# The layer norm ahead of the expert stage, with its last tile centred early and its mean spread beside the root

## The chip, the cores and the metric

One Trainium2 chip, one NeuronCore of it. The metric is the device time of one execution in microseconds; lower is better. Before the change, three runs gave 3672.79 us as the median (3670.61 to 3675.13).

## What is computed

Two blocks of a network on 512 tokens of width 1024, in float32. The first block has two layers, each with two SwiGLU feed-forward parts and a token mixer of gated MLP, differential attention and sparse attention. The second block is one layer: a second token mixer, a layer norm, an expert stage (PEER: 8 heads choose 16 of 16,384 experts for each token) and a last layer norm. The change concerns the first layer norm of the second block and the start of the expert stage behind it:

```python
def layer_norm(x, g, b):
    mu = jnp.mean(xf, axis=-1, keepdims=True)
    xc = xf - mu
    var = jnp.mean(xc * xc, axis=-1, keepdims=True)
    return xc * lax.rsqrt(var + LN_EPS) * g + b

x = layer_norm(DEEPNORM_ALPHA * x + m, ln1_g[l], ln1_b[l])   # m: the mixer's output
f = peer_ffn(x, ...)                                         # begins with q = x @ wq
```

## The kernel before

Activations lie transposed: `self.x[k]` (k = 0 to 7) holds 128 channels on the partitions and 512 tokens along the free axis. Sums over channels are therefore sums over partitions and over the eight tiles. Every float32 product is made of three matmuls of split operands: a weight tile is loaded into `raw` by SyncE's DMA queue, ScalarE rounds it into a high part (`wh`, line 260), VectorE subtracts to get the low part (`wl`, line 261), and activations are split in the same way into `yh` and `yl` (lines 266 and 267). `raw` has four buffers, `wh` and `wl` three each. A scheduler of the framework lays out each engine's queue at build time and sets the semaphores; on the chip each queue runs in that fixed order.

The stage around the change runs as follows.

- In `mix2`, the output projection gives one tile of 128 channels after another: 24 matmuls of 512 columns each (line 283), then VectorE adds the result to `ALPHA * x[d]` (line 1542). `centre` (lines 1244 to 1261) subtracts a provisional mean `cen`, which was taken from tiles 0 and 1, from each tile as it comes; ScalarE squares it (line 1258), and VectorE adds the tile and its square to the running tiles `csum` and `csq` (lines 1260 and 1261). Behind the last projection, three weight units of the expert stage's first product (`heads`, from `wq`) are loaded and split ahead of time (`unit`).
- `moments` (line 1263) lets PE sum `csum` and `csq` over the partitions with a column of ones, four matmuls of one column for each; a float32 matmul appears as two passes in the trace. VectorE works out mean `lnm` and variance `lnv` on 128x4 tiles, and `rsqrt` (line 318) makes the inverse root from a bit trick and three Newton steps, nine small instructions on `rst` and `rsy`.
- `normed` (line 1278) spreads two 512-token rows over all partitions by matmuls with the identity (`spread`, line 348): the inverse root `rsy` and the product of mean and root, `lnmr`. For each tile k, ScalarE makes `e = -g*lnmr + b` (line 1289), VectorE `y = x*g*rsy` (line 1291) and `x = y + e` (line 1293).
- In `peer`, ScalarE and VectorE split each normalized tile into `yh` and `yl`, and PE adds its nine matmuls (three heads, three parts each; `mm3`, lines 271 to 273) into three PSUM banks. Two of these banks come free only when the two spread rows have been read to the end. PE also transposes all tiles to token rows (32 matmuls of 128 columns, line 1780), which ScalarE copies out (line 1781); then it copies the heads' results (`x<-proj`, line 1610), which frees the banks for the dense expert products (line 283 again).

Of the kernel before, what the change touches and what calls it, by code (L numbers as in the profile page):

```python
# [10 lines left out]
F32 = mybir.dt.float32  # L11
# [4 lines left out]
AF = mybir.ActivationFunctionType  # L16
OP = mybir.AluOpType
AX = mybir.AxisListType

P = 128  # L20
S = 512
D = 1024
KT = D // P
NT = S // P
# [7 lines left out]
ALPHA = 2.0 ** 0.25  # L32
# [161 lines left out]
class Net:  # L194
# [58 lines left out]

    def unit(self, src, n=1024):
        nc = self.nc
        raw = self.rawp.tile([P, 1024], F32, name="raw", tag="raw")
        nc.sync.dma_start(raw[:, :n], src)
        h = self.wp.tile([P, 1024], F32R, name="wh", tag="wh")
        l = self.wp.tile([P, 1024], F32R, name="wl", tag="wl")
        nc.scalar.activation(h[:, :n], raw[:, :n], AF.Copy)  # L260
        self.latest = nc.vector.tensor_sub(l[:, :n], raw[:, :n], h[:, :n].bitcast(F32)).ins  # L261
        return h, l
# [997 lines left out]
                nc.vector.tensor_add(self.csum, self.csum if k > 1 else self.x[0], x)  # L1260
                nc.vector.tensor_add(self.csq, self.csq, sq)

    def moments(self):

        nc = self.nc
        ps = self.bank("stat")
        for i, v in enumerate((self.csum, self.csq)):
            for t in range(NT):
                nc.tensor.matmul(ps[:, i * NT + t:i * NT + t + 1], lhsT=v[:, t * P:(t + 1) * P],
                                 rhs=self.ones[:, :1], start=True, stop=True)  # L1270
        m, v, q = (self.sm(NT, n, bufs=1) for n in ("lnm", "lnv", "lnq"))
        nc.vector.tensor_scalar(m, ps[:, :NT], 1.0 / D, None, op0=OP.mult)
        nc.vector.tensor_scalar(v, ps[:, NT:2 * NT], 1.0 / D, LN_EPS, op0=OP.mult, op1=OP.add)
        nc.vector.tensor_mul(q, m, m)
        nc.vector.tensor_sub(v, v, q)
        return self.rsqrt(v, NT), m

    def normed(self, st, g, b, out, mk):

        nc = self.nc  # L1280
        r, m = st
        mr = self.sm(NT, "lnmr", bufs=1)
        nc.vector.tensor_mul(mr, m, r)
        rb, mb = self.spread(r), self.spread(mr)
        ng = self.sm(KT, "lnng", bufs=1)
        nc.vector.tensor_scalar(ng, g, -1.0, None, op0=OP.mult)
        for k in range(KT):
            e = mk("lne")
            nc.scalar.activation(e, mb, AF.Identity, scale=ng[:, k:k + 1], bias=b[:, k:k + 1])
            y = mk("lny")  # L1290
            nc.vector.scalar_tensor_tensor(y, self.x[k], g[:, k:k + 1], rb, op0=OP.mult, op1=OP.mult)
            o = out(k)
            nc.vector.tensor_add(o, y, e)
            yield k, o

    def mix2(self, begun):
        nc, A = self.nc, self.A
        X, begun = begun
        self.main = "T"
        vec = self.blk(name="vec2")  # L1300
        o = 0
        V = {}
        for n, w in (("convw", 62), ("convb", 2), ("nag", 2), ("nab", 2), ("pools", 2), ("convc", 6)):
            V[n] = vec[:, o:o + w]
            src = A[n]
# [218 lines left out]
        rb = self.layer_norm(H, 256)  # L1524
# [4 lines left out]
        for a in range(2):  # L1529
            y = self.t32("y")  # L1530
# [4 lines left out]
        attend(1)  # L1535

        Y = YB + YC + YA + YD
        for d in range(KT):
            ps = self.proj(A["wout2"][d], Y)
            if d == KT - 1:  # L1540
                heads = [self.unit(A["wq"][i].rearrange("p k m -> p (k m)")) for i in range(3)]
            nc.vector.scalar_tensor_tensor(self.x[d], self.x[d], ALPHA, ps, op0=OP.mult, op1=OP.add)
            self.centre(d - 1)
        self.centre(KT - 1)
        return self.moments(), heads

    def top16(self, vals, n, out, idx):

# [197 lines left out]
    def peer(self, out, begun):  # L1746
        nc, A = self.nc, self.A
# [5 lines left out]
        n, last, early = S - GT, len(BLOCKS) - 1, GT // P  # L1753
# [7 lines left out]
        ln = cst[:, 384:400].rearrange("p (a b) -> p a b", a=2)  # L1761
# [5 lines left out]
        XT = [self.cact] + [stage.tile([P, D], F32, name=f"xt{t}", tag=f"xt{t}") for t in range(1, NT)]  # L1767
        stats, heads = begun
        X, begun = [], [self.bank("proj") for _ in heads]
        for k, x in self.normed(stats, ln[:, 0], ln[:, 1], lambda k: self.x[k], self.t32):  # L1770
            X.append(self.new_pair())
            self.split(x, *X[k])
            c = slice(k * P, (k + 1) * P)
            for ps, (h, l) in zip(begun, heads):
                self.mm3(ps, h[:, c], l[:, c], *X[k], k == 0, k == KT - 1)
# [66 lines left out]
        while not over or kept % 2:  # L1842
            g = self.t32("hg")[:, GT:]
# [8 lines left out]
        for j in range(kept, NE):  # L1852
# [6 lines left out]
            hi, lo = (v[:, :n] for v in self.new_pair())  # L1859
# [6 lines left out]
        for i in range(4):  # L1866
            src = A["ln2"][i // 2, i % 2 * S:(i % 2 + 1) * S]
# [121 lines left out]
```

## Time and profile before

| | |
|---|---|
| median of three runs | 3672.79 us |
| the profiled execution | 3671.99 us |
| its span, first to last instruction | 3670.2 us |
| PE busy | 3554.5 us |
| VectorE (DVE) busy | 2394.7 us |
| ScalarE (ACT) busy | 1562.9 us |
| mean granted TensorE clock | 0.988 of full speed |

The profile is of one execution on the chip. PE is TensorE's matmuls, PEld its weight loads, DVE VectorE, ACT ScalarE, POOL GpSimd, and SPq, ACTq and POOLq the queues' own work (DMA issues). All moments are microseconds from the span's start; a duration behind an instruction is how long it ran. Matmuls overlap: of a row with eight matmuls the time runs from the first start to the last end. Idle time in brackets names what the engine waited for, and on which line that was made.

### The profile page before, as it was taken

How to read it: one execution, taken by the hardware profiler on the slowest of the kernel's cores; microseconds unless marked ns; L12 is line 12 of the kernel's file. 1: busy time of each engine (PE TensorE's matmuls, PEld its weight loads, DVE VectorE, ACT ScalarE, POOL GpSimd, SP SyncE). 2: the span in 40 equal slices, each digit the busy share in tenths (PEclk: the TensorE clock that was granted, in tenths of full speed). 3: DMA queues.
4: the chain of work that ended last, by engine and by line, in shares of the span. 5: the costliest groups of instructions: out<-in, count | busy, mean ns of one | idle time of the engine just before them, and what ended most of it. 6: DMA issues, size and time to landing. Idle time of an engine off the chain costs nothing. (4 is left out here: it accounts for less than half of the span.)

```text
span 3670.2 us, 49271 instructions
## 1 busy us (share of the span) xinstructions
PE 3554.5 (97%) x18265; PEld 3019.0 (82%) x18265; DVE 2394.7 (65%) x4791; ACT 1562.9 (43%) x2769; POOL 369.2 (10%) x358
## 2 busy tenths in 40 slices
PE   7999999999999999999999999899899999999998
PEld 6888876788888888767888887788899999988786
DVE  6555687665563334776533386699877667778787
ACT  4332366433233323465432263433667753334333
POOL 0000100000000001000000000021221134432220
PEclk9999999999999999999999999999999999999999
DMA  7666320266653333401333322265686879999995
GB/s 249 190 186 198 115 94 18 64 202 193 201 178 109 94 95 105 133 24 31 91 98 93 97 79 68 84 202 195 206 289 235 296 262 308 313 327 346 336 341 183
DMA packets 259665, 635.72 MB, mean 173 GB/s; under 512 B 82336, under 2 KB 117584, under 8 KB 256864
## 3 DMA queue, kind: packets, MB, share of 16 engines
q1 hardware_dynamic: 206368, 473.96, 40.1%
q0 software_dynamic: 39808, 140.52, 11.2%
q10 hardware_dynamic: 13248, 18.09, 1.3%
q8 instruction: 143, 2.34, 0.3%
q14 instruction: 98, 0.80, 0.1%
HBM read 591.32 MB, written 41.16 MB: 172 GB/s over the span
## 5 line engine op out<-in xcount | busy, mean ns | idle before, releaser
L260 ACT ACTIVATE wh<-raw 128x1024 fp32r<-128x1024 f32 (+2 forms) x620 | 645.3, 1043 | 1129.3 <-PE proj L283 880.6
L261 DVE TENSOR_TENSOR wl<-raw,wh 128x1024 fp32r<-128x1024 f32 (+2 forms) x620 | 744.1, 1201 | 508.4 <-ACT wh L260 370.1
L283 PE MATMUL proj<-yh,wh 128*128 128x512 f32 (+1 forms) x2744 | 644.7, 375 | 9.1 <-ACT hg L1839 4.2
L283 PE MATMUL proj<-yh,wl 128*128 128x512 f32 (+1 forms) x2744 | 629.1, 371 | 13.6 <-DVE wl L261 13.6
L283 PE MATMUL proj<-yl,wh 128*128 128x512 f32 (+1 forms) x2744 | 628.4, 370 | 0.0
L283 PEld LDWEIGHTS proj<-yh,wl 128*128 128x128 f32 x2744 | 506.4, 189 | 82.8 <-DVE wl L261 15.5
L283 PEld LDWEIGHTS proj<-yh,wh 128*128 128x128 f32 x2744 | 501.1, 189 | 85.0 <-ACT hg L1839 5.7
L283 PEld LDWEIGHTS proj<-yl,wh 128*128 128x128 f32 x2744 | 505.4, 189 | 67.5
L535 DVE SCALAR_TENSOR_TENSOR scr<-raw,cact 128x1024 bf16<-128x1024 f32 x128 | 156.7, 1224 | 136.3 <-DMA raw<-in_wada 136.0
L1822 PE MATMUL acc<-wl,yh 128*128 128x512 f32 x756 | 236.2, 394 | 2.7 <-DVE wl L261 2.6
L1822 PE MATMUL acc<-wh,yh 128*128 128x512 f32 x756 | 235.0, 392 | 3.6 <-ACT yh L266 2.1
L1822 PE MATMUL acc<-wh,yl 128*128 128x512 f32 x756 | 234.3, 391 | 0.3 <-DVE yl L267 0.3
L1737 POOL DMA_INDIRECT row<-in_purows,c x128 | 156.5, 1223 | 537.9 <-DVE row L1721 261.6
L667 DVE TENSOR_TENSOR ga<-sg,proj 128x512 f32<-128x512 f32 x88 | 60.5, 687 | 225.7 <-PE proj L283 223.2
L1737 POOL DMA_INDIRECT row<-in_pv,c x128 | 165.2, 1291 | 392.6 <-DVE vacc L1729 275.8
L272 PE MATMUL proj<-yl,wh 128*128 128x256 f32 (+1 forms) x552 | 177.0, 330 | 10.6 <-DVE yl L394 7.0
L273 PE MATMUL proj<-yh,wl 128*128 128x256 f32 (+1 forms) x552 | 174.6, 324 | 2.2 <-DVE wl L261 2.2
L1822 PEld LDWEIGHTS acc<-wl,yh 128*128 128x128 f32 x756 | 141.1, 188 | 38.4 <-DVE wl L261 9.5
L271 PE MATMUL proj<-yh,wh 128*128 128x256 f32 (+1 forms) x552 | 164.8, 328 | 7.8 <-ACT yh L640 6.3
L1822 PEld LDWEIGHTS acc<-wh,yh 128*128 128x128 f32 x756 | 142.1, 189 | 32.0 <-ACT yh L266 2.5
L1822 PEld LDWEIGHTS acc<-wh,yl 128*128 128x128 f32 x756 | 142.5, 189 | 31.4 <-DVE yl L267 1.0
L1729 DVE SCALAR_TENSOR_TENSOR vacc<-row,act,vacc 128x1024 f32<-128x1024 f32 x127 | 162.5, 1280 | 0.6
(465 smaller groups left out, 5166.7 us busy)
## 6 DMA issues: line engine op xcount, KB each, us to landing
raw<-in_wada SPq DMA_DIRECT2D x144, 512.0 KB
raw<-in_pu SPq DMA_DIRECT2D x128, 512.0 KB
raw<-in_pv SPq DMA_DIRECT2D x128, 512.0 KB
raw<-in_wg SPq DMA_DIRECT2D x84, 512.0 KB
raw<-in_wu SPq DMA_DIRECT2D x84, 512.0 KB
raw<-in_wd SPq DMA_DIRECT2D x64, 512.0 KB
gates<-st SPq DMA_DIRECT2D x20, 1024.0 KB
acts<-hg ACTq DMA_DIRECT2D x92, 192.0 KB
```

What stands on the lines that cost most here:

```text
L260: nc.scalar.activation(h[:, :n], raw[:, :n], AF.Copy)
L261: self.latest = nc.vector.tensor_sub(l[:, :n], raw[:, :n], h[:, :n].bitcast(F32)).ins
L271: mm(out, lhsT=lh, rhs=rh, start=start, stop=False)
L272: mm(out, lhsT=lh, rhs=rl, start=False, stop=False)
L273: mm(out, lhsT=ll, rhs=rh, start=False, stop=stop)
L283: self.nc.tensor.matmul(ps, lhsT=w[:, k * P:(k + 1) * P], rhs=X[c + k][part], start=c + k + i == 0, stop=i == 2 and c + k == nk - 1)
L535: nc.vector.scalar_tensor_tensor(scr, raw, 1.0, self.cact, op0=OP.mult, op1=OP.mult, accum_out=self.mod[:, l, j:j + 1])
L667: nc.vector.tensor_mul(a, sg, p[1])
L1729: nc.vector.scalar_tensor_tensor(acc, row, a, acc, op0=OP.mult, op1=OP.add)
L1737: nc.gpsimd.indirect_dma_start(out=row, out_offset=None, in_=tables[kind], in_offset=bass.IndirectOffsetOnAxis(ap=self.experts[:GT, s:s + ...
L1822: nc.tensor.matmul(acc[q], lhsT=a[:, t * P:(t + 1) * P], rhs=half(w, m), start=q not in started, stop=end and i == 2)
```

## The change

- The last tile, `x[7]`, is scaled by `ALPHA` and centred in one VectorE instruction as soon as `cen` is known, while PE still works on earlier tiles. When its projection is done, one add is left on VectorE and one square on ScalarE; the tile and its square are not added to `csum` and `csq`.
- `moments` sums `csum` and the last tile, and `csq` and the last square, on PE: 16 one-column matmuls in place of 8.
- Of the third head unit, only the load of `raw` stays in place (`raw`); the split (`unit_of`) is put behind the end of the root (`issue_after`).
- `normed` spreads the mean itself, not its product with the root, so that spread comes ahead of the root's end. VectorE subtracts the spread mean from each tile, then multiplies by `g` and the spread root; ScalarE adds the bias twice, once rounding into the high part `yh`, once into `x`; VectorE subtracts for `yl`. The instruction for `e`, the add into `x` and the separate split are gone.

```diff
-    def moments(self):
+    def moments(self, x, sq):
...
-        for i, v in enumerate((self.csum, self.csq)):
+        for i, vs in enumerate(((self.csum, x), (self.csq, sq))):
             for t in range(NT):
-                nc.tensor.matmul(ps[:, i * NT + t:i * NT + t + 1], lhsT=v[:, t * P:(t + 1) * P],
-                                 rhs=self.ones[:, :1], start=True, stop=True)
+                for n, v in enumerate(vs):
+                    nc.tensor.matmul(ps[:, i * NT + t:i * NT + t + 1], lhsT=v[:, t * P:(t + 1) * P],
+                                     rhs=self.ones[:, :1], start=n == 0, stop=n == 1)
...
-    def normed(self, st, g, b, out, mk):
+    def normed(self, st, g, b):
...
-        mr = self.sm(NT, "lnmr", bufs=1)
-        nc.vector.tensor_mul(mr, m, r)
-        rb, mb = self.spread(r), self.spread(mr)
-        ng = self.sm(KT, "lnng", bufs=1)
-        nc.vector.tensor_scalar(ng, g, -1.0, None, op0=OP.mult)
-        for k in range(KT):
-            e = mk("lne")
-            nc.scalar.activation(e, mb, AF.Identity, scale=ng[:, k:k + 1], bias=b[:, k:k + 1])
-            y = mk("lny")
-            nc.vector.scalar_tensor_tensor(y, self.x[k], g[:, k:k + 1], rb, op0=OP.mult, op1=OP.mult)
-            o = out(k)
-            nc.vector.tensor_add(o, y, e)
-            yield k, o
+        mb, rb, left = self.spread(m), self.spread(r), []
+        for k in range(KT + 2):
+            if k < KT:
+                left.append(self.t32("lny"))
+                nc.vector.tensor_sub(left[k], self.x[k], mb)
+            k -= 2
+            if k >= 0:
+                y, (hi, lo) = left[k], self.new_pair()
+                nc.vector.scalar_tensor_tensor(y, y, g[:, k:k + 1], rb, op0=OP.mult, op1=OP.mult)
+                for o in (hi, self.x[k]):
+                    nc.scalar.activation(o, y, AF.Identity, bias=b[:, k:k + 1])
+                nc.vector.tensor_sub(lo, self.x[k], hi.bitcast(F32))
+                yield k, (hi, lo)
...
-        for d in range(KT):
-            ps = self.proj(A["wout2"][d], Y)
-            if d == KT - 1:
-                heads = [self.unit(A["wq"][i].rearrange("p k m -> p (k m)")) for i in range(3)]
-            nc.vector.scalar_tensor_tensor(self.x[d], self.x[d], ALPHA, ps, op0=OP.mult, op1=OP.add)
+        stt = nc.vector.scalar_tensor_tensor
+        for d in range(KT - 1):
+            stt(self.x[d], self.x[d], ALPHA, self.proj(A["wout2"][d], Y), op0=OP.mult, op1=OP.add)
             self.centre(d - 1)
-        self.centre(KT - 1)
-        return self.moments(), heads
+        self.centre(KT - 2)
+
+        x, sq = self.x[KT - 1], self.t32("sq")
+        stt(x, x, ALPHA, self.cen, op0=OP.mult, op1=OP.subtract)
+        ps = self.proj(A["wout2"][KT - 1], Y)
+        heads = [self.unit(A["wq"][i].rearrange("p k m -> p (k m)")) for i in range(2)]
+        raw = self.raw(A["wq"][2].rearrange("p k m -> p (k m)"))
+        nc.vector.tensor_add(x, x, ps)
+        nc.scalar.activation(sq, x, AF.Square)
+        st = self.moments(x, sq)
+        with self.tc.issue_after(self.rooted):
+            heads.append(self.unit_of(raw))
+        return st, heads
```

Three places in the queues show what the scheduler made of it. In these rows `x_87` to `x_94` are the tiles 0 to 7, and the lines are those of each version's own file.

VectorE ahead of the statistics (`lnm` is the first instruction behind PE's sums), before:

```order
L261 TENSOR_TENSOR wl<-raw,wh 128x1024
L1542 SCALAR_TENSOR_TENSOR x_94<-x_94,proj 128x512
L1256 TENSOR_TENSOR x_94<-x_94,cen 128x512
L1260 TENSOR_TENSOR csum<-csum,x_94 128x512
L1261 TENSOR_TENSOR csq<-csq,sq 128x512
L1272 TENSOR_SCALAR lnm<-stat 128x4
```

and with the change:

```order
L1264 TENSOR_TENSOR x_93<-x_93,cen 128x512
L1268 TENSOR_TENSOR csum<-csum,x_93 128x512
L1269 TENSOR_TENSOR csq<-csq,sq 128x512
L1558 TENSOR_TENSOR x_94<-x_94,proj 128x512
L1281 TENSOR_SCALAR lnm<-stat 128x4
```

Of the five wide instructions ahead of `lnm`, one is left behind the last projection; the rows on `x_93` run while PE still works on it.

VectorE from the first Newton step on, with the change (before, the nine rows of the root stand together, and the `CAST` follows them):

```order
L343 SCALAR_TENSOR_TENSOR rsy<-rst,rsy 128x4
L1295 TENSOR_TENSOR lny<-x_87,spread 128x512
L341 TENSOR_TENSOR rst<-rsy,lnv 128x4
L1295 TENSOR_TENSOR lny<-x_88,spread 128x512
L342 TENSOR_TENSOR rst<-rst,rsy 128x4
L1778 CAST iota_19135<-pcst 128x512
L343 SCALAR_TENSOR_TENSOR rsy<-rst,rsy 128x4
L1295 TENSOR_TENSOR lny<-x_89,spread 128x512
...
L1295 TENSOR_TENSOR lny<-x_91,spread 128x512
L343 SCALAR_TENSOR_TENSOR rsy<-rst,rsy 128x4
L269 TENSOR_TENSOR wl<-raw,wh 128x1024
L1295 TENSOR_TENSOR lny<-x_92,spread 128x512
```

Five wide subtractions and the `CAST` of a constant table now stand between the steps of the root, and the third unit's low part with a sixth subtraction between the root and the first multiplication. The subtraction of tile 7 stands nine rows further on, in the midst of the multiplications.

ScalarE at the end of the stage, before:

```order
L266 ACTIVATE yh<-x_94 128x512
L260 ACTIVATE wh<-raw 128x1024 x2
L1781 ACTIVATE cact<-xt 128x512
L1781 ACTIVATE xt_19134<-xt 128x512
L1781 ACTIVATE xt_19135<-xt 128x512 x2
L1781 ACTIVATE xt_19136<-xt 128x512 x2
L1610 ACTIVATE x_91<-proj 128x512
```

and with the change:

```order
L1301 ACTIVATE yh<-lny,pcst 128x512
L268 ACTIVATE wh<-raw 128x1024 x3
L1798 ACTIVATE cact<-xt 128x512
L1798 ACTIVATE xt_19140<-xt 128x512 x2
L1798 ACTIVATE xt_19141<-xt 128x512 x2
L1798 ACTIVATE xt_19142<-xt 128x512 x2
L1628 ACTIVATE x_91<-proj 128x512
```

Three weight splits, not two, stand ahead of the copies, and seven copies, not six, ahead of the heads' first result. On PE, 4 of the 32 transposes now stand among the heads' matmuls and 28 behind them; before, 13 and 19. PE takes the first head's tiles 0 to 3, one high matmul of tile 4, then the second head from tile 0 on.

## Rows read from the trace of the kernel before

**Rows 1.** The page: the span, and PE's busy time, share, instructions.

```profile
span 3670.2 us, 49271 instructions
PE 3554.5 (97%) x18265; PEld 3019.0 (82%) x18265; DVE 2394.7 (65%) x4791; ACT 1562.9 (43%) x2769; POOL 369.2 (10%) x358
```

**Rows 2.** Windows of the norm: busy us (instructions) by engine, then granted clock, DMA.

```profile
2320.00:2324.80 4.80, 1.38 (x13) 1.32 (x12) 3.87 (x5) 0.63 (x1) 0.00 (x0) 1.00 0.38 109
2325.00:2331.50 6.50, 3.51 (x17) 3.46 (x18) 3.64 (x21) 0.00 (x0) 1.06 (x2) 0.50 0.17 52
2335.30:2338.50 3.20, 3.05 (x8) 2.13 (x8) 3.20 (x6) 2.78 (x5) 0.00 (x0) 0.50 0.02 5
2342.00:2356.00 14.00, 14.00 (x65) 11.55 (x64) 4.98 (x9) 4.06 (x7) 0.00 (x0) 1.00 0.00 0
```

**Rows 3.** Timeline, last projection to the statistics: start, us, engine, line, out<-in.

```profile
2316.27 1.98 PE L283 MATMUL proj<-yl,wh 128*128 128x512 f32 x8
...
2318.09 1.97 PE L283 MATMUL proj<-yh,wl 128*128 128x512 f32 x8
...
2320.16 1.23 DVE L261 TENSOR_TENSOR wl<-raw,wh 128x1024 fp32r<-128x1024 f32 x1 [1.68 <-PE proj L283]
2321.30 0.68 DVE L1542 SCALAR_TENSOR_TENSOR x<-x,proj 128x512 f32<-128x512 f32 x1
...
2323.49 1.05 PE L1269 MATMUL stat<-ones,csum 128*128 128x1 f32 x8 [3.42 <-DVE csum L1260]
...
2324.40 1.36 PE L1269 MATMUL stat<-ones,csq 128*128 128x1 f32 x8
2325.80 0.16 DVE L1272 TENSOR_SCALAR lnm<-stat 128x4 f32<-128x4 f32 x1 [1.70 <-PE stat L1269]
```

**Rows 4.** The same timeline, root and spread.

```profile
2326.30 0.53 POOL L1758 DMA_DIRECT2D pcst<-in_iota  x1 [196.95 <-DVE lnq L1274]
...
2328.44 0.16 DVE L335 SCALAR_TENSOR_TENSOR rsy<-rst,rsy 128x4 f32<-128x4 f32 x1
...
2328.75 2.05 PE L352 MATMUL spread<-ident,rsy 128*128 128x128 f32 x8 [2.99 <-DVE rsy L335]
2328.89 0.43 DVE L1760 CAST iota<-pcst 128x512 bf16<-128x512 f32 x1 [0.29 <-DMA pcst<-in_iota]
...
2330.83 1.41 DVE L1291 SCALAR_TENSOR_TENSOR lny<-x,pcst,spread 128x512 f32<-128x512 f32 x2 [1.36 <-PE spread L352]
```

**Rows 5.** Groups by line and shape: count, busy us, mean ns of one, idle before.

```profile
L1289 ACT ACTIVATE lne<-spread,pcst,lnng 128x512 f32<-128x512 f32 x8 | 5.8, 769 | 8.9 <-DVE lny L1291 8.9
L267 DVE TENSOR_TENSOR yl<-x,yh 128x512 fp32r<-128x512 f32 x8 | 5.5, 686 | 0.7 <-ACT yh L266 0.7
L266 ACT ACTIVATE yh<-x 128x512 fp32r<-128x512 f32 x8 | 5.1, 632 | 3.5 <-DVE x L1293 3.5
L1416 ACT ACTIVATE se<-se,one 128x512 f32<-128x512 f32 x10 | 6.4, 713 | 0.0
```

**Rows 6.** The same timeline, end of the stage.

```profile
2354.86 2.01 ACT L260 ACTIVATE wh<-raw 128x1024 fp32r<-128x1024 f32 x2 [7.95 <-PE proj L272]
...
2356.25 2.29 PE L1780 MATMUL xt<-ident,x 128*128 128x128 f32 x19
2356.77 0.57 ACT L1781 ACTIVATE cact<-xt 128x512 f32<-128x512 f32 x1
...
2357.25 2.53 ACT L1781 ACTIVATE xt<-xt 128x512 f32<-128x512 f32 x5
2359.63 1.62 ACT L1610 ACTIVATE x<-proj 128x512 f32<-128x512 f32 x3
...
2360.32 1.70 PE L283 MATMUL proj<-yh,wh 128*128 128x384 f32 x8 [1.78 <-ACT x L1610]
```

**Rows 7.** The same timeline: two matmuls of the heads in the slow stretch.

```profile
2336.37 0.63 PE L273 MATMUL proj<-yh,wl 128*128 128x512 f32 x1
...
2336.80 0.63 PE L271 MATMUL proj<-yh,wh 128*128 128x512 f32 x1
```

More of the change, by code (lines that the diff above doesn't have):

```diff
@@ L255, in unit, with raw, unit_of @@
         nc = self.nc
+        raw = self.raw(src, n)
+        return self.unit_of(raw, n)
+    def raw(self, src, n=1024):
         raw = self.rawp.tile([P, 1024], F32, name="raw", tag="raw")
-        nc.sync.dma_start(raw[:, :n], src)
+        self.nc.sync.dma_start(raw[:, :n], src)
+        return raw
+    def unit_of(self, raw, n=1024):
+        nc = self.nc
         h = self.wp.tile([P, 1024], F32R, name="wh", tag="wh")
@@ L1769, in peer @@
         X, begun = [], [self.bank("proj") for _ in heads]
-        for k, x in self.normed(stats, ln[:, 0], ln[:, 1], lambda k: self.x[k], self.t32):
-            X.append(self.new_pair())
-            self.split(x, *X[k])
+        for k, pair in self.normed(stats, ln[:, 0], ln[:, 1]):
+            X.append(pair)
             c = slice(k * P, (k + 1) * P)
```

## The prediction

> **What bounds the kernel now.** I read the page first: PE is busy for 97% of the span [rows 1], so time is to be had only where PE stands still. The windows and the timeline of the norm show such a place. PE's last projection matmul ends at 2318.09 + 1.97 = 2320.06 [rows 3]; in the 4.8 us that follow PE is busy for 1.38 us, in the next 6.5 us for 3.51 us at a granted clock of 0.50 (1.2 GHz), and only from 2342 to 2356 does it work without a gap at 1.00 (2.4 GHz) [rows 2]. Moments below are given without the leading 23, so 20.06 is 2320.06.
>
> The reader should follow one chain. DVE takes a weight's low part first, then four instructions on the last tile, until PE starts the sums at 23.49; they end at about 25.76, and `lnm` starts at 25.80 [rows 3]. The root ends at 28.44 + 0.16 = 28.60, PE spreads the root, and the first wide multiplication starts at 30.83 [rows 4], 10.8 us after the projection. From there the tiles come one by one: DVE does three instructions on each, ACT two [rows 5]. PE's first head can only run tile by tile; the second needs the bank of a spread row. In the timeline PE is without gaps from 41.37 on, with 60 of the 72 head matmuls and 9 transposes left, until the last head matmul at 56.25. Then follow 19 transposes while ACT splits two units, makes six copies and takes the first head out of its bank, and PE goes on at 60.32 [rows 6]. That restart, 40.26 us after the projection's end, is what the change has to bring forward. The work behind it is bound by PE again, so I carry a shift there to the end one for one.
>
> **The change, part by part.** I walk the new queues with these durations.
>
> *Tail of the last tile.* Gone from behind the projection are the third unit's low part (20.16 to 21.30), the centring and two sums. Left is one add: it starts at about 20.10, as the low part did, and its result is ready at 20.79 (0.68 us, as line 1542) [rows 3]. The square on ACT runs beside PE's first sums: 0.63 us like line 266 [rows 5]. The early scaling and centring of tile 7 is one more wide DVE instruction (0.69 us) in a stretch where DVE is not full; PE's 24 matmuls for each remaining projection (5.5 us at 0.2275 [rows 3]) hide it; without that cover it would cost its 0.7 us.
>
> *Sums by PE.* 16 matmuls are 32 passes, not 16. The passes on `csum` start 0.91 us before those on `csq`, eight of them: 0.114 us each; the `csq` group takes 1.36 us for eight, 0.17 each [rows 3], where the clock fell. One matmul on `csum` can go ahead of the add, so 30 passes remain from 20.84 on: 3.4 us at the fast price, 5.1 at the slow one. The sums end between 24.4 and 26.0. I take 0.12 a pass, near the fast end, because in the window up to 24.8 the clock was still 1.00 after an idle stretch [rows 2], and now PE works in it. So `lnm` starts at 24.6, **1.2 us earlier**: of the 3.4 us taken out ahead of the sums, 2.2 go back into the sums themselves.
>
> *Mean spread beside the root.* PE can spread `lnm` from 24.85. A spread ran 2.08 us from its first pass to the first reader (28.75 to 30.83) at clock 0.50 [rows 2, 4]; at full clock it is no less than half, 1.04. The first Newton step ends at 24.6 + 1.65 = 26.25, so the first subtraction starts between 26.3 and 26.9; I take 26.3, with the clock still up behind the sums. Now the remaining six small root steps wait between wide instructions: 5 subtractions at about 0.62 us start to start (5.5 us for eight of line 267 [rows 5] is 0.69 each with overlap at the seams taken off), the cast of 0.43 [rows 4] and six small steps at about 0.1. The root ends near 26.3 + 3.1 + 0.4 + 0.6 = 30.4, **1.8 us later than before**. The cast needs its table from POOL's DMA, which waits for the end of the sums: before, it was issued at 26.30 and the cast ran at 28.89, 3.1 us behind `lnm` [rows 4]; DVE will now reach it about 3.3 us behind `lnm`, so it is just there. If it came 1 us late, the root and all behind it would wait that long.
>
> PE then spreads the root, 2.08 us at the slow clock or 1.04 at the fast. I take the slow one, since PE has nothing to do between the two spreads for about four microseconds, and before, 2.99 us of idle time stood ahead of the spread at clock 0.50 [rows 2, 4]. Meanwhile DVE does the third unit's low part (1.23) and the sixth subtraction, so both are hidden. The first multiplication starts at **32.6**, 1.8 us later than before.
>
> *The tile loop.* But DVE now has 8 multiplications, 8 splits and only two subtractions behind it, where it had 24 wide instructions. ACT does two passes of a tile with one bias column: 0.713 us alone, 0.64 in a row (6.4 us for ten of line 1416 [rows 5]), between line 266's 0.632 and line 1289's 0.769. 16 passes and one copy make 10.8 us, to about 44. Interleaved by their queues, DVE's subtraction of tile 7 ends at 39.9, which frees the second head's bank, and the last multiplication at 42.5, which frees the third's. PE has by then done tiles 0 to 3 of the first head and one matmul of tile 4, 13 matmuls in all, waiting for ACT in between, and runs without gaps from **40.0**. 59 matmuls remain: 16.27 to 18.09 for eight [rows 3] is 0.2275 each, 13.4 us. They end at 53.4, **2.8 us earlier** than before; 1.0 us of this is only that the nine transposes (0.12 us each, 2.29 us for 19 [rows 6]) now stand behind.
>
> *The end of the stage.* There ACT has three splits to do in place of two before it may copy, and seven copies in place of six. A split adds half of 2.01 us, 0.96 start to start with the overlap off; a copy (59.63 - 56.77)/6 = 0.48 [rows 6]. Before, the restart came 60.32 - 56.25 = 4.07 us behind the last head matmul; now 4.07 + 0.96 + 0.48 = 5.5, at 58.9. **The sum: 60.3 - 58.9 = 1.4 us gained.** With both spreads at the slow price it is 0.8, with both at the fast 2.0.
>
> *Queues.* The third unit's `raw` buffer is given back about 10 us later, so one load of expert weights and, behind it on SyncE, the load of the keys start that much later, near 31. The weights are wanted by ACT at about 52 and the keys behind the heads' copies, near 70: nothing waits. POOL's DMA keeps its place.
>
> The profiled execution took 3671.99 us, so I predict **3670.6 us**. That execution lies 0.8 us below the median of the runs shown, 3672.79, and the runs spread by 2.2 and 2.3 us to both sides of it. A difference under 0.2%, 7.3 us, is taken as no change throughout.
>
> **The rivals.** *More is gained.* The clock stays up at both spreads (0.6 more), and ACT's third split does not hold up the copies (1.4 more): 3671.99 - 3.4 = 3668.6. For it speaks that the sums now fill PE's first hole; against it ACT's queue as the scheduler wrote it.
>
> *No gain.* The sums run at 0.17 a pass, as `csq` did, and `lnm` starts at 26.0. The 1.4 us are gone: 3672.0. The change would then shorten DVE's tail and lengthen PE's by the same.
>
> *Slower.* The heads run at the slow clock. Their matmuls stood 0.43 us apart in the slow stretch (36.37 to 36.80 [rows 7]), against 0.2275: 0.2 us lost for each. The mechanism lies at the start of the first head, where tiles reach PE one by one from ACT, about 1.28 us apart, with three matmuls each. The gain is used up when seven of the 59 matmuls behind 40.0 run slow; with 16 the time is 3671.99 - 1.4 + 3.2 = 3673.8, with all 59 3682.4. Before, the clock came back after 3.2 us of nearly full work at 0.50 [rows 2], and a first head whose tiles come 1.28 us apart keeps a slow PE nearly as full (three times 0.43), so I hold a short delay possible and a long one unlikely. The Trainium skill, "TensorE: Matmul & The Clock Gate", section "Why this matters for your kernels", says that idle gaps between bursts of matmuls send PE back to half rate. That speaks against this change: the pause between the two spreads is longer than any that the norm had before. By that rule the second spread, and the start of the heads, run slow; the fall to 0.50 after the first hole agrees.
>
> *Much is gained.* The whole difference between PE's idle time and its work between 20.06 and 41.37 is 18.1 us (21.3 less 3.2 us for 12 head matmuls and 4 transposes); a gain above 7.3 us needs two fifths of it. No step of the walk gives that, since root, spread and the first tile still stand one behind the other.
>
> **How the numbers follow.** The forecast with its bounds of 0.8 and 2.0 has 0.55, more gain 0.16, no gain 0.12, slower 0.13, much gain 0.04. The range reaches from the third case less the runs' spread, 3668.6 - 2.2 = 3666.4, to the slow case with 16 matmuls plus it, 3673.8 + 2.2 = 3676.0; the tails beyond hold the two far cases. Faster than 0.2%: 0.04 for much gain and 0.01 for the edge of more gain, 0.05. Slower than 0.2% needs some 43 slow matmuls: 0.03 of the 0.13. No change: 0.92.
>
> **What would show it.** In the new trace: `lnm` 4.5 us behind the projection's end, not 5.7; the root's last step about 5.8 us behind `lnm`, not 2.6; the first multiplication near 12.5 us behind the projection, not 10.8; heads without gaps from about 20 us behind it, not 21.3; the restart 5.5 us behind the last head matmul. I am wrong if the sums take over 5 us, if DVE stands still before the cast, if the clock is 0.50 behind the 20 us point, or if a shift of the restart does not reach the end.

## The result, and the profile after

The change takes 3722.05 us (median of 6 runs, 3709.43 to 3728.32) against 3674.14 us for the kernel before beside it (6 runs, 3670.61 to 3679.39): a ratio of 1.0125, 95% interval 1.0106 to 1.0143. The prediction was no change, 3670.6 us, with a range up to 3676.0.

The page of the changed kernel, its span and PE's busy time, against [rows 1]:

```profile
span 3723.4 us, 49302 instructions
...
PE 3606.1 (97%) x18281; PEld 3020.4 (81%) x18281; DVE 2391.9 (64%) x4787; ACT 1563.4 (42%) x2769; POOL 373.3 (10%) x358
```

The span is 53.2 us longer, and PE is busy 51.6 us longer, with 16 more matmul records in 18,265. So PE hardly waited more: its instructions took longer. The timeline shows when. In the changed kernel the last projection ahead of the norm and `lnm` read (start us, duration, engine, line, out<-in):

```profile
2353.92 2.03 PE L291 MATMUL proj<-yl,wh 128*128 128x512 f32 x8
2355.79 2.03 PE L291 MATMUL proj<-yh,wl 128*128 128x512 f32 x8
...
2363.33 0.16 DVE L1281 TENSOR_SCALAR lnm<-stat 128x4 f32<-128x4 f32 x1 [4.79 <-PE stat L1278]
```

The projection ends at 2357.82, 37.8 us later than the 2320.06 of before, though ahead of this point only the handling of the last tile was rewritten (one VectorE instruction of 0.68 us brought forward). Eight matmuls now take 1.87 us start to start, where [rows 3] has 1.82. The groups by line and shape show how far this reaches (count, busy us, mean ns of one, idle before); line 283 of before is line 291 now, and 1822 is 1839. First the kernel before:

```profile
L283 PE MATMUL proj<-yl,wh 128*128 128x512 f32 x1720 | 426.3, 390 | 0.0
...
L1822 PE MATMUL acc<-wh,yl 128*128 128x512 f32 x756 | 234.3, 391 | 0.3 <-DVE yl L267 0.3
...
L283 PE MATMUL proj<-yl,wh 128*128 128x384 f32 x1024 | 202.1, 337 | 0.0
L283 PE MATMUL proj<-gh,wh 128*128 128x512 f32 x616 | 153.3, 389 | 0.0
```

and the change:

```profile
L291 PE MATMUL proj<-yl,wh 128*128 128x512 f32 x1720 | 436.7, 396 | 0.0
...
L1839 PE MATMUL acc<-wh,yl 128*128 128x512 f32 x756 | 235.6, 393 | 1.4 <-DVE yl L275 1.4
...
L291 PE MATMUL proj<-yl,wh 128*128 128x384 f32 x1024 | 204.5, 340 | 0.0
...
L291 PE MATMUL proj<-gh,wh 128*128 128x512 f32 x616 | 157.4, 396 | 0.0
```

In the mean, a 512-column matmul of line 283 costs 5 to 7 ns more. Over the six such groups (three as the first row with 1720 each, three as the last with 616) the busy time rises from 1743.6 to 1788.3 us, 44.7 us; the three groups of 384 columns add 4.9, the three of line 1839 3.3, together 52.9 us. Against them the six groups of 256 columns on lines 271 to 273 fell by 5.0 us and small shifts elsewhere remain, so these groups make up nearly all of the span's 53.2 us, not exactly all. The norm isn't where the time went.

What the text of the change moved unseen are the tiles. It no longer makes `lnmr` and `lnng`, two tiles of the pool `small`, each in a slot of 32 bytes a partition. (A pool is a stretch of the on-chip memory from which the framework hands out tiles.) The pools lie one behind the other, so all tiles of the pools behind `small` start 64 bytes lower in the built program: the activation tiles (`yh`, `yl`, `gh`, `gl`) at 103872 + 2048n in place of 103936 + 2048n. The split weights `wh` and `wl` of the weight pool lie ahead of it and stayed (57856 and 70144, in steps of 4096). Two fills set the starts. `PAD`, the width in float32 columns of an unused tile in `small`, moves the activation tiles alone; the 120 of the unused tile `pad2`, ahead of all these pools, moves the weights and all that lies behind them.

### The profile page after: what moved, and what is told of

The parts are those of the page before. It is cut to its first block, busy times and chain, and to the rows that moved or that the text cites. A ratio compares the mean times of both kernels' runs of the same rounds, so it can differ in the third digit from the quotient of the medians.

```text
span 3723.4 us, 49302 instructions
## 1 busy us (share of the span) xinstructions
PE 3606.1 (97%) x18281; PEld 3020.4 (81%) x18281; DVE 2391.9 (64%) x4787; ACT 1563.4 (42%) x2769; POOL 373.3 (10%) x358
## 5 line engine op out<-in xcount | busy, mean ns | idle before, releaser
L291 PE MATMUL proj<-yh,wh 128*128 128x512 f32 (+1 forms) x2744 | 655.6, 379 | 8.7 <-ACT hg L1856 4.0
L291 PE MATMUL proj<-yh,wl 128*128 128x512 f32 (+1 forms) x2744 | 642.7, 376 | 15.9 <-DVE wl L269 15.9
L291 PE MATMUL proj<-yl,wh 128*128 128x512 f32 (+1 forms) x2744 | 641.2, 375 | 0.0
```

Source lines behind the costliest of these rows:

```text
L291: self.nc.tensor.matmul(ps, lhsT=w[:, k * P:(k + 1) * P], rhs=X[c + k][part], start=c + k + i == 0, stop=i == 2 and c + k == nk - 1)
```

## Experiments: the place of the tiles

PE has two operands on line 283: it loads a 128-column slice of the weight tile and streams a 512-column activation tile. "Distance" below is the start of the first streamed tile less that of the first loaded one, less 46080, its value before (180 times 256); the other tiles lie whole multiples of 512 bytes from these. The starts of all these tiles come from the built programs. In all runs of this section the engines' queues are those of the kernel that the run is made from, but for the fills. Each ratio is to runs of the kernel before that were taken beside it.

**The change with its tiles put back**

```diff
-PAD = 40
+PAD = 56
```

> The change as it stands, with 64 bytes a partition of padding put back ahead of the tiles of the phase pool (pad3 56 columns, not 40), so that these tiles start at 103936 as before the change and not at 103872. No queue differs from the changed kernel but for one memset's width. Placement theory: the matmuls of line 291 with 512 columns go back from 0.2333 us start to start to 0.2269, and the time to that of the kernel before less the gain of the norm's walk, 3671 to 3674 us. Rival, that the norm's new instructions and order cost the time: 3722 us as with the change.

Measured: 3673.12 us (11 runs, 3663.11 to 3677.97), ratio 0.9984 (0.9972 to 0.9995). With 64 bytes of fill the loss is gone.

**The kernel before with its tiles 64 bytes lower**

```diff
-PAD = 40
+PAD = 24
```

> The kernel before, with 64 bytes a partition of padding taken away (pad3 24 columns, not 40), so that the phase tiles start at 103872 as with the change; nothing of the norm is changed. Placement theory: 7008 matmuls of 512 columns at 6.4 ns more each and 3072 of 384 columns at some 2.6 ns more, 45 + 8 = 53 us: about 3725 us. Rival, that the norm's new order costs the time: 3674 us, as before.

Measured: 3722.58 us, ratio 1.0120 (1.0105 to 1.0136): the loss without the change. Its timeline shows whose time it is:

```profile
1900.01 1.23 DVE L261 TENSOR_TENSOR wl<-raw,wh 128x1024 fp32r<-128x1024 f32 x1 [3.16 <-ACT wh L260]
...
1901.62 2.03 PE L283 MATMUL proj<-yl,wh 128*128 128x512 f32 x8
...
1903.49 1.80 PE L283 MATMUL proj<-yh,wl 128*128 128x512 f32 x7
1903.73 1.06 ACT L260 ACTIVATE wh<-raw 128x1024 fp32r<-128x1024 f32 x1 [3.18 <-PE proj L283]
```

The eight matmuls from 1901.62 to 1903.49 take 1.87 us although no instruction of VectorE, ScalarE or GpSimd runs beside them. A load of weights does run there (the DMA share of that stretch is 0.65). So look at the heads' matmuls in the norm, where in two stretches nothing runs beside PE, loads included. First the changed kernel, then the change with its tiles put back (a window of each, in the form of [rows 2], and its first and last matmul):

```profile
2386.16:2391.95 5.79, 5.79 (x26) 4.67 (x25) 0.00 (x0) 0.00 (x0) 0.00 (x0) 1.00 0.00 0
2386.16 0.39 PE L281 MATMUL proj<-yh,wl 128*128 128x512 f32 x1
...
2391.76 0.39 PE L281 MATMUL proj<-yh,wl 128*128 128x512 f32 x1
```

```profile
2352.62:2358.00 5.38, 5.38 (x25) 4.48 (x24) 0.00 (x0) 0.00 (x0) 0.00 (x0) 1.00 0.00 0
2352.62 0.39 PE L279 MATMUL proj<-yh,wh 128*128 128x512 f32 x1
...
2357.83 0.39 PE L281 MATMUL proj<-yh,wl 128*128 128x512 f32 x1
```

24 steps take 5.60 us, 0.2333 each, in the first; 23 steps take 5.21 us, 0.2265 each, in the second. PE is slower by itself, at a granted clock of 1.00.

**128 bytes lower**

```diff
-PAD = 40
+PAD = 8
```

> The kernel before, with 128 bytes of padding taken away (pad3 8 columns): the phase tiles start at 103808, a multiple of 128 bytes but not of 256. If what counts is a 128-byte boundary: 3674 us, as before, and 0.2269 us a matmul. If it is a boundary of 256 bytes or more: about 3725 us. Rival, that only the amount taken away counts, whatever the boundary: more than 3725 us.

Measured: 3717.15 us, ratio 1.0117 (1.0101 to 1.0132). A boundary of 128 bytes does not help.

**The weight pools 64 bytes higher, the activation tiles where they were**

```diff
-        self.pad(c, "pad2", 120)
+        self.pad(c, "pad2", 136)
-PAD = 40
+PAD = 24
```

> The kernel before, with 64 bytes more padding ahead of the pools of loads, split weights and temporaries and 64 bytes less ahead of the phase tiles: the weight tiles start 64 bytes past a 128-byte boundary, the phase tiles stay at 103936. If only the operand that streams through PE counts: the projections (phase tiles streamed) keep 0.2269 us, and only matmuls that stream a weight tile slow down, the 2268 of line 1822 and some 400 others, 6.4 ns each: about 17 us, 3691 us. If the stationary operand counts: the projections slow down too and the time is 3720 us or more. If neither: 3674 us.

Measured: 3715.92 us, ratio 1.0111 (1.0096 to 1.0127). The streamed tiles stood on their old place, a multiple of 512, and were slow all the same. So I formed a theory of the distance.

**Both 64 bytes higher**

```diff
-        self.pad(c, "pad2", 120)
+        self.pad(c, "pad2", 136)
```

> The kernel before, with the weight pools AND the phase tiles 64 bytes higher, so that their distance is as before while neither stands on a multiple of 512. Before, line 283's eight matmuls of 512 columns take 1.813 us start to start (0.2267 each); with the phase tiles alone 64 lower, and with the weight tiles alone 64 higher, 1.867 (0.2333), and both cost about 1.1%. Theory R (only the distance between the streamed activation tile and the weight tile that is loaded beside it counts): 0.2267 each and 3676 +- 5 us, no difference from before. Rival A (each tile's own place counts): at least 0.2333 each and 3716 us or more; were the two losses of separate kinds and added, 0.240 each and some 3760.

Measured: 3676.87 us, ratio 1.0003 (0.9994 to 1.0013). No operand stands on its old boundary, and nothing is lost:

```profile
L283 PE MATMUL proj<-yl,wh 128*128 128x512 f32 x1720 | 426.3, 390 | 0.0
...
L1822 PE MATMUL acc<-wh,yl 128*128 128x512 f32 x756 | 234.3, 391 | 2.7 <-DVE yl L267 2.7
```

The rival of the places themselves falls.

**The activation tiles alone 64 and 256 bytes higher** (`PAD = 56` and `PAD = 104`, one run each)

> The kernel before, with the phase tiles alone 64 bytes higher. 64 lower gave 0.2333 us a matmul on line 283. Theory R: a distance of +64 is another one than -64, so the price may differ, but it isn't 0.2267; 0.230 to 0.240 and 3700 to 3760 us. Rival A (a tile off its boundary costs, whichever way): 0.2333 and 3716 to 3723. If it is 0.2267, one direction is free and both theories are too simple.

> The kernel before, with the phase tiles alone 256 bytes higher. At -128 line 283 took 0.2325 us a matmul, at -64 0.2333. If a boundary of 256 bytes is enough: 0.2267 and 3671 to 3680 us. If the pattern is that of the 512-byte slices in which the weights are loaded: 0.230 to 0.233 and 3700 to 3720 us.

Measured: 3698.11 and 3673.1 us. At +64:

```profile
L283 PE MATMUL proj<-yl,wh 128*128 128x512 f32 x1720 | 431.5, 393 | 0.0
...
L1822 PE MATMUL acc<-wh,yl 128*128 128x512 f32 x756 | 238.6, 397 | 1.8 <-DVE yl L267 1.8
```

Line 283 lost half as much as at -64, and a matmul of line 1822, which had lost 2 to 3 ns there, now lost 6. At +256 both stand as before.

**32 bytes lower** (`PAD = 32`, one run)

> The kernel before with the phase tiles 32 bytes lower. Line 283's matmul of 512 columns took 0.2267 us at a distance of 0 and of 256 bytes, 0.2333 at -64, 0.2325 at -128, 0.2288 at +64. If the price rises with the distance: between 0.2267 and 0.2333, about 0.230, and 3690 to 3700 us. If any distance that is no multiple of 256 costs the same on the low side: 0.2333 and 3716 to 3723. If 32 bytes are within one step of the memory: 0.2267 and 3671 to 3680.

Measured: 3732.59 us, in one run, above all four at -64 (3715.00 to 3730.89). Line 283 pays the same as there, line 1822 more; the price doesn't rise with the distance:

```profile
L283 PE MATMUL proj<-yl,wh 128*128 128x512 f32 x1720 | 437.3, 396 | 0.0
...
L1822 PE MATMUL acc<-wh,yl 128*128 128x512 f32 x756 | 238.7, 397 | 3.1 <-DVE yl L267 3.1
```

**The split weights alone.** In the run with the weight pools moved, `raw` and the temporaries of VectorE and ScalarE had moved too. Here a 64-byte fill stands ahead of `wh` and `wl`, and one of 192 behind them:

```diff
         self.pad(c, "pad0", 96)
+        self.pad(self.wp, "pad4", 16)
+        self.pad(self.tmp, "pad5", 48)
```

> The kernel before with the split weight tiles wh and wl 64 bytes higher and the raw weights where they were; VectorE's and ScalarE's temporaries and the phase tiles 256 bytes higher, a shift that cost nothing for the phase tiles alone. So of the tiles that move, only those that PE loads for line 283 have another distance modulo 256 to the rest. Theory R (the streamed activation tile against the loaded weight tile, both PE's own): streamed minus loaded is -64, line 283 at 0.2333 us a matmul, 3712 to 3722 us, as with all weight pools 64 higher. Rival (PE's reads against VectorE's, ScalarE's and the loads' accesses to raw weights and temporaries): those have kept their distances to the activation tiles, so 0.2267 and 3676 +- 5 us.

Measured: 3717.73 us, ratio 1.0128 (1.0104 to 1.0151).

```profile
L283 PE MATMUL proj<-yl,wh 128*128 128x512 f32 x1720 | 437.4, 396 | 0.0
...
L1822 PE MATMUL acc<-wh,yl 128*128 128x512 f32 x756 | 235.7, 393 | 1.1 <-DVE yl L267 1.1
```

So of all that moved, the distance between PE's own two operands decides.

**The change as it is, its weights moved after its activations**

```diff
-        self.pad(c, "pad2", 120)
+        self.pad(c, "pad2", 104)
-PAD = 40
+PAD = 56
```

> The change with its phase tiles left where it put them (64 bytes lower than before), and the weight pools moved 64 bytes lower too, so that only the distance of before is restored. Theory R (the distance between streamed and loaded tile): line 291's matmuls of 512 columns at 0.2267 us each and 3673 +- 4 us, as when the phase tiles were moved back. Rival A (the places themselves, off a multiple of 512): 0.2333 or more and 3716 us or more. The time is also a second measurement of what the norm's part is worth: if that is a gain that can be measured, the ratio's interval lies below 1 again; if it is nothing, as the stage in the traces says (PE's restart 40.65 us behind the last projection, 40.26 before), it takes in 1.

Measured: 3675.18 us (11 runs, 3672.16 to 3680.22), ratio 1.0003 (0.9993 to 1.0013), line 291's group at 426.2 us and 390 ns. Together:

| distance, bytes | kernels | line 283 `yl,wh`, mean ns | line 1822 `wh,yl`, mean ns |
|---|---|---|---|
| 0 | before; both +64; the change, put back in two ways | 390 | 390 to 392 |
| +256 | before +256 | 390 | 392 |
| -32 | before -32 | 396 | 397 |
| -64 | the change; before -64; weights +64 | 396 | 393 to 394 |
| +192 (256 more) | split weights +64, activations +256 | 396 | 393 |
| -128 | before -128 | 395 | 397 |
| +64 | before +64 | 393 | 397 |

On line 1822 PE loads activation slices and streams weights, so its pairs see the distance with the other sign. That fits its prices at -64 and +64, which are line 283's turned round; no run moved its tiles apart from line 283's.

## Experiments: the stage

With the distance restored the stage can be read by itself. Moments in us behind the end of the last projection (the first row from [rows 3, 4, 6], the others from the same rows of each trace):

| | `lnm` | root's end | first multiplication | transposes begin | PE's restart |
|---|---|---|---|---|---|
| before | 5.7 | 8.5 | 10.8 | 36.2 | 40.3 |
| predicted | 4.5 | 10.3 | 12.5 | 33.3 | 38.8 |
| the change | 5.5 | 11.8 | 14.0 | 35.6 | 41.0 |
| the change, activations put back | 5.3 | 11.7 | 13.8 | 35.1 | 40.65 |
| the change, weights moved after | 5.4 | 11.7 | 13.9 | 35.2 | 40.7 |
| subtractions behind the root | 5.4 | 8.3 | 11.5 | 34.8 | 40.3 |
| the same with idle matmuls | 4.3 | 7.2 | 10.4 | 32.8 | 38.3 |

The kernel before, in the runs at distance 0 and +256, restarted at 40.3, 41.7 and 40.2: two executions of one stage lie as far apart as the whole gain that was forecast (1.4 us). So no gain of the stage is to be seen. The change with its activations put back, by windows (busy us of PE, PEld, DVE, ACT, POOL with instructions, then granted clock, DMA share, GB/s):

```profile
2324.28:2327.30 3.02, 2.35 (x21) 2.27 (x22) 0.69 (x1) 0.63 (x1) 0.00 (x0) 1.00 0.00 0
2327.30:2344.40 17.10, 10.96 (x40) 8.87 (x40) 13.27 (x34) 5.01 (x8) 1.06 (x2) 0.50 0.18 51
...
2345.70:2359.40 13.70, 13.70 (x60) 11.32 (x61) 4.54 (x8) 5.72 (x9) 0.00 (x0) 1.00 0.00 0
```

The clock falls in the midst of the sums and stays at 0.50 (1.2 GHz) for 17.1 us, up to 20.1 behind the projection. In its profile the kernel before had 0.50 for 6.8 us, 1.00 for 3.4 and 0.50 for 3.4 more:

```profile
2325.00:2331.80 6.80, 3.81 (x18) 3.75 (x19) 3.94 (x21) 0.00 (x0) 1.06 (x2) 0.50 0.17 49
2331.80:2335.20 3.40, 1.29 (x7) 0.68 (x5) 2.54 (x5) 2.91 (x5) 0.00 (x0) 1.00 0.00 0
2335.20:2338.60 3.40, 3.25 (x8) 2.23 (x8) 3.40 (x6) 2.88 (x5) 0.00 (x0) 0.50 0.02 5
```

Two suspects, then: the root, which waits between wide subtractions, and the clock.

**The subtractions behind the root**, on the change with its activations put back:

```diff
-                nc.vector.tensor_sub(left[k], self.x[k], mb)
+                with self.tc.issue_after(self.rooted): nc.vector.tensor_sub(left[k], self.x[k], mb)
```

> The change with its tiles back in place (the last experiment on it: lnm 5.3 us behind the last projection, the root's end 11.5 behind it, the first multiplication 13.8, PE's restart on the expert products 40.65; before the change 5.7, 8.5, 10.8 and 40.26), and with the wide subtractions of the mean put behind the root instead of between its steps. Theory (the loss in the stage is the root's, which waits between wide instructions on VectorE): root 8.2 behind the projection, first multiplication 11.8, restart 38.6 to 39.7, so 1 to 2 us better than the change in the stage; the whole 3671 +- 4 us. Rival (ScalarE's sixteen passes and the copies at the end bind, or the slow clock in the heads): the first multiplication comes earlier but the restart stays within 0.4 us of 40.65; 3673 +- 4 us.

Measured: 3673.55 us, ratio 0.9995 (0.9986 to 1.0004). Root and first multiplication come 3.3 and 2.3 us earlier, the restart 0.3: the rival's result. The root's wait between wide instructions was real, but not what sets the restart. In its timeline

```profile
2332.58 0.74 DVE L1299 SCALAR_TENSOR_TENSOR lny<-lny,pcst,spread 128x512 f32<-128x512 f32 x1
...
2336.43 0.63 PE L281 MATMUL proj<-yh,wl 128*128 128x512 f32 x1
2336.85 0.63 PE L279 MATMUL proj<-yh,wh 128*128 128x512 f32 x1
```

PE has its tiles but runs its head matmuls 0.42 us apart, at clock 0.50 up to 2341.0, 19.95 behind the projection.

**Idle matmuls behind the spread of the root**, on that version:

```diff
+        with self.tc.issue_after(self.rooted): [nc.tensor.matmul(self.fill[0], lhsT=self.fill[1][:, :P], rhs=self.fill[1][:, :S], start=True, stop=True) for _ in range(6)]
```

> The version with the subtractions behind the root, and six idle matmuls of 512 columns behind the spread of the root, into the first head's bank, which its first real matmul clears again. Without them the clock was 0.50 for 17 us, up to 19.9 us behind the last projection, PE worked without a gap at half speed from 14.8 us on, and the restart came at 40.31. Theory (the slow clock in the heads is what took the expected gain): with PE full from the first spread on, the clock is back before the first head's first tiles, 13 to 16 us behind the projection, and the restart comes 0.5 to 1.2 us earlier, 39.1 to 39.8; the whole 3672 +- 4 us. Rival (the chain of tiles on VectorE and ScalarE and the banks bind whatever the clock is): clock back early, restart within 0.3 us of 40.31. Third: the six matmuls run slow (0.43 us each, 2.6 us) without bringing the clock back, and the restart is as late or later.

Measured: 3672.99 us, ratio 0.9996 (0.9984 to 1.0007).

```profile
2324.80:2331.60 6.80, 6.32 (x22) 5.30 (x22) 6.38 (x21) 0.31 (x1) 0.99 (x2) 0.52 0.34 105
2331.60:2339.30 7.70, 5.06 (x18) 2.57 (x17) 7.70 (x14) 6.25 (x11) 0.00 (x0) 1.00 0.06 21
```

The clock is back 11.5 us behind the projection, and the restart comes at 38.3. Of the 2.0 us, 1.1 are not the idle matmuls': in this execution the clock held through the sums ahead of them, and `lnm` stood at 4.3. From `lnm` to the restart it is 34.0 against 34.9 us, 0.9 gained, within the theory's 0.5 to 1.2, in one trace of each. But the profile shows where it goes next:

```profile
2358.45 2.78 PE L291 MATMUL proj<-yh,wh 128*128 128x384 f32 x8 [1.78 <-ACT x L1628]
2361.03 2.03 PE L291 MATMUL proj<-yl,wh 128*128 128x384 f32 x8
2362.90 1.55 PE L291 MATMUL proj<-yh,wl 128*128 128x384 f32 x8
...
2359.00:2362.20 3.20, 3.20 (x11) 3.20 (x11) 0.00 (x0) 0.38 (x1) 0.00 (x0) 0.52 0.29 111
```

Behind the restart two groups of eight run slow, 2.78 and 2.03 us where [rows 6] has 1.70 and later groups 1.55: 1.6 us are given back. The window shows why (busy us, then granted clock): the clock fell again, to 0.52 in the mean of 2359.00 to 2362.20, with PE busy throughout. The same stands in the run without idle matmuls (2.78 and 2.03 us, clock 0.50), and not in the three traces of the change itself (1.66 to 1.68 us for the first eight; clock 1.00 in the one with the activations put back). There too 28 transposes and PE's pauses of 0.19 and 1.78 us stand ahead of the restart; what decides whether the clock falls is open. So no version here is shown to beat the kernel before.

## Why the prediction was wrong

- **The step that failed** stands ahead of all terms: "I walk the new queues with these durations." Every duration outside the norm was carried over, and the two vanished tiles `lnmr` and `lnng` were put at nothing without a reason. Without them the operands of 7008 matmuls of 512 columns stand at a distance at which each costs 6.4 ns more: 44.7 us in the profile, where 48 us were lost between the medians. None of the four rivals had a mechanism outside the stage, so the range missed by 46 us.
- **For the norm alone the forecast of no change holds, but not by its working.** With the distance restored the ratio is 0.9984 (0.9972 to 0.9995) and 1.0003 (0.9993 to 1.0013), both within 0.2% of none; 3673.1 and 3675.2 us lie in the range. The first interval alone excludes 1; the stage in its trace shows no gain that would explain it, and the second measurement doesn't repeat it. That the range holds here says little: it is wider than the forecast gain, and so are the intervals.
- **The 1.4 us of gain in the stage did not come.** With the activations put back the restart came 1.8 us behind the forecast: 0.8 at `lnm`, 0.5 from there to the root's end, 0.5 from the first multiplication to the transposes. `lnm` was due at 4.5 and came at 5.3 to 5.5: "I take 0.12 a pass ... now PE works in it". In the changed kernel two passes took 0.22 us, close to the 0.24 taken, up to 2360.40, and 0.43 from 2360.63 on, where the clock had fallen although PE was busy:

```profile
2357.82:2360.60 2.78, 2.12 (x20) 2.03 (x20) 0.69 (x1) 0.63 (x1) 0.00 (x0) 1.00 0.00 0
2360.60:2363.30 2.70, 2.70 (x14) 2.61 (x13) 0.00 (x0) 0.00 (x0) 0.00 (x0) 0.51 0.00 0
...
2360.40 0.36 PE L1278 MATMUL stat<-ones,sq 128*128 128x1 f32 x2
2360.63 0.53 PE L1278 MATMUL stat<-ones,csq 128*128 128x1 f32 x2
...
2362.73 0.57 PE L1278 MATMUL stat<-ones,sq 128*128 128x1 f32 x2
...
2363.71 2.05 PE L360 MATMUL spread<-ident,lnm 128*128 128x128 f32 x8 [0.41 <-DVE lnq L1283]
...
2365.80 0.69 DVE L1295 TENSOR_TENSOR lny<-x,spread 128x512 f32<-128x512 f32 x1 [0.73 <-PE spread L360]
```

- **The root** was due 5.8 us behind `lnm` and ended 6.3 behind it: the first spread ran at the slow price, so the first subtraction started 2.5 us behind `lnm`, not 1.7. The cast did not wait, as forecast.
- **Heads without gaps** came at 21.4 behind the projection, not 20 (with activations put back), and the transposes at 35.1, not 33.3. 5.5 us from the last head matmul to the restart, with three splits and seven copies, was right (5.5 in that run, too). The rival "no gain" named the outcome and a part of its cause: only the last sums ran at its slow price. The slow clock in the heads, of the rival "slower", took part; its price of some 2 us is less than these runs can tell.
- **Two sums** in the walk don't come out, without weight for the result. The tail took 2.65 us out ahead of PE's sums (23.49 to 20.84) and some 1.5 went back into them; 3.4 and 2.2 give the same 1.2. And with the second spread at full clock the gain is not 2.0: behind the root VectorE's low part and sixth subtraction, 1.23 + 0.62 us, would then end last, so only some 0.3 us come on top of the 1.4.

## What to carry to other kernels

Where pools lie one behind the other, as here, a change that adds or drops a tile, however small, moves the tiles of every pool behind it; compare the addresses of the built program before costing anything, and keep the distance of PE's two operands with a fill. When matmuls far from an edit change their mean by a few ns in the groups by line, look at the places of the tiles first. A shorter chain on one engine brought nothing here, because the next one, PE at half clock, was then late.

## What was unexpected of the hardware

- A matmul of 512 columns (operands split from float32) took 0.227 us start to start or up to 0.233, by the distance of the streamed from the loaded tile alone: free at 0 and 256 bytes, 3 to 6 ns more in line 283's mean at -32, -64, -128, +64 and +192. Why is open; that the reads of the two operands meet is argued, not shown. The Trainium skill, "SBUF — State Buffer", section "SBUF: two separate sides", says that PE never waits on anyone and that on the engines' side only the port shared by VectorE and GpSimd causes contention. That leaves no room for a price by place, and the measurement differs: PE is slowed here by its own operands, with no other engine and no load at work (0.2333 us a step in the stretch from 2386.16). The same page's "Operand start alignment" asks for a multiple of the element's size, which all these places are; it speaks of legality alone.
- Matmuls of 256 columns went the other way: in the changed kernel, at -64, those of line 271 fell from 286 to 284 ns, of line 272 from 292 to 290, of line 273 from 285 to 282.
- PE's clock fell to 0.50 behind a stretch in which PE was busy 2.35 of 3.02 us, mostly with one-column matmuls. The Trainium skill, "TensorE: Matmul & The Clock Gate", section "Why this matters for your kernels", has idle gaps between bursts as the cause. Here it fell with PE at work, the longest pause in that stretch 0.67 us, while in the run with idle matmuls the same sums ran at 1.00 to their end (PE busy 3.62 of 4.32 us); what decides it is open.
